# Rows of w_o loaded and split in a lane beside the gated unit, a tenth gate pair by seven products, and order and paces reset, in a hybrid S5 and mLSTM block

## The chip, the cores and the metric

The kernel runs on one core of a Trainium2 chip. The metric is the time of one execution on the device, in microseconds (us), taken as the median of several runs. Besides the runs there is one profiled execution, from which the page of the profile and all answers of the trace come. Engines are named as in the profile: PE (matmul), PEld (its weight loads), DVE (vector), ACT (scalar), POOL, SP (which issues most DMAs; SPq is its queue).

## The reference, cut to what matters

One decoder block on 1024 positions plus 16 learned meta positions, width 1024, all in float32:

```python
h = layer_norm(concat(meta, x))
p = h @ w_in + b_in        # u_s5 | q | k | v | o | i | f | g_s5 | g_m
y_s5 = GLU(gelu(S5(u_s5))) # z = gelu(y) @ s5_w_glu; z[:, :D] * sigmoid(z[:, D:])
y_m  = (sigmoid(o) * head_norm(mLSTM(q, k, v, i, f))) @ m_w_out
mix  = sigmoid(g_s5) * y_s5 + sigmoid(g_m) * y_m
h    = layer_norm(ALPHA * h + mix @ w_o)
h    = layer_norm(ALPHA * h + relu(h @ w_up + b_up)**2 @ w_down)
```

The output leaves out the meta positions.

## The kernel before, in words

Every product keeps float32 accuracy by splitting both operands into a high and a low part (type fp32r) and adding three matmuls: high by high (L274), low by high or high by low (L275, L276), in the helper `mm3`. A weight tile of 128x1024 (512 KB) is loaded by a DMA into `wraw`, copied on ACT to its high part (`whi`, rounded) and subtracted on DVE to its low part (`wlo`). All such tiles are slots of one pool, `big`, with 30 slots; a load can be issued only when the slot that it takes is free.

The program runs a list of jobs, one after the other on PE: first LN0 and the first jobs, in an order written out by hand; then those of the string `ORDER`. In it `q`, `v`, `u`, `o` are plain jobs of the first projection (`o0` to `o7` the output gate's tiles of 128 columns). The gates (o, g_s5, g_m) can also be taken in pairs of tiles by seven products in place of eight (Strassen's scheme in Winograd's form): pair p has a first part `a`p (`ga_job`, three products; ACT and DVE split the raw weights into `gmwh`/`gmwl`, DVE makes sums of weights, `wus`, at L1472 to L1475, of which one is split into `gmo`) and a second part `b`p (`gb_job`, four products). Between the two, weights' sums lie in DRAM (`gw_dr`) and partial results in `e_dr`, and are fetched again; only pairs that are among the last three `a` and the first three `b` stay in SBUF (`HELD`). Pairs 0 to 3 are the tiles of o, 4 to 7 those of g_s5, 8 to 11 those of g_m. `G_E` and `G_L` are lists of pairs whose split of the weights is written earlier, or whose third operand is written later.

After `ORDER` come `ym0` to `ym7` (the product with m_w_out) and `glu` to `glu7`, the gated unit, whose evacuation on ACT (`z2s`, L1087) and DVE (L1091 to L1093) ends in `mixr`. It reads two of the four batches of gelu(y) from rows 7 and 6 of the buffer `hT_hi`/`hT_lo` (`GROW`), which before held h transposed. Then comes the product with w_o: its eight rows of 128x1024 are loaded into `woraw` (L1606) and split into the eight rows of the same buffer (L1607 on ACT, L1608 on DVE); `mix` is split into `mxh` (L1620, ACT) and `mxl` (L1621, DVE), 64 pieces of 128x128 each; LN1 follows, then the feed-forward (up by seven products, down), and LN2.

Beside the jobs run lanes: generators for work that feeds other stages (mLSTM `ml`, S5 `s5`, `s5c`, `s5g`; the scaled residual `ah_scale`; the gate on the mLSTM's result `hm_gate`; the first up weights `up_early`, which writes split sums `wpre` and stores them in `wu_dr`). `LANE_AT` says at which job a lane begins, `PACE` how fast it goes against PE's clock, which `mm3` counts. In the S5 lane the 64 results `s5z` (64x130) go from PSUM to `s5Z` by ACT (L917) or DVE (L915); with `ZD = 1` every second one is on DVE. A scheduler then sets the final order of each engine from this program text.

Of the kernel before, what the change touches and what calls it, by code (L numbers as in the profile page):

```python
# [12 lines left out]
AF = mybir.ActivationFunctionType  # L13
OP = mybir.AluOpType
P = 128

D = 1024
KT = D // P
# [19 lines left out]
LN2_1 = 0.693359375  # L38
LN2_2 = math.log(2.0) - LN2_1
MAGIC = 1.5 * 2 ** 23  # L40
ORDER = 'q1 q0 v0 v1 q3 q2 o3 v2 a3 o0 u0 u1 v3 o2 o4 o5 u2 o1 a4 a6 a7 u3 a11 a8 a9 a5 a10 b9 b10 b5 b4 b3 b6 b8 b11 b7'
HS = 3
GH = 3
HOLD = 3
# [1 line left out]
TFA = 1  # L46
TLA = 1
T_UP = 100
REST = 11.83
G_E = [5, 10]  # L50
G_L = [5]
HGD = 1
UPD = 1
TPW = 5.29
S5_START = 'o3'
LANE_AT = {'t_prep': 'q0', 'hm_gate': 'a8', 'hmo': 'b7', 'ah_scale': 'ym5', 'up_early': 'glu3'}
PACE = {'ml': 0.56, 'cv': 0.104, 's5': 1.103, 's5c': 0.683, 's5g': 3.512, 'ah': 1.602, 'up': 1.036, 'hg': 1.92, 'hn': 1.0, 'hm': 0.66}
UP = {'ml': 10, 'cv': 0, 's5': 0, 's5c': 0, 's5g': 0, 'ah': 0, 'up': 0, 'hg': 0, 'hn': 0, 'hm': 0}
SPLIT_UP = 0
PRE = 3  # L60
UP_AT = (0, 1, 4, 6)
ZD = 1
ML = [1.912, 1.186, 1.815, 10.865]
NL = [0.584, 3.726, 10.192, 11.252]
B5 = [16, 0.1, 0.1, 50]
C5 = [0.84, 0.798, 1.345, 4.956]
K5 = [1.652, 1.0, 8.0, 0.475]
Z5 = [2.284, 1.264, 0.394, 0.269]
D5 = [3.696, 1.28, 1.716, 0.267]
W5 = [5.284, 0.829, 15.575, 0.848]  # L70
Y5 = [0.792, 1.657, 4.502, 6.57]
CV0 = 0
HRA = 1
A_AFT = 0
# [71 lines left out]
def decoder_block(  # L146
# [4 lines left out]
    nc = tc.nc  # L151
    v_, a_, g_, t_ = nc.vector, nc.scalar, nc.gpsimd, nc.tensor
# [9 lines left out]
    def slot(name, dt=F32):  # L162
        return big.tile([P, SLOT], dt, tag="s", name=name)
# [7 lines left out]
    def f32(ap):  # L171
        return ap.bitcast(F32)
# [3 lines left out]

    lanes = {n: Lane(p, tc, UP.get(n, 0)) for n, p in PACE.items()}
    clock = [0.0]
# [59 lines left out]
    def split_w(job, later=False):  # L238
        if later:
            return split_now(job, True)  # L240
        with tc.high_priority(offset=SPLIT_UP):
            split_now(job)
# [258 lines left out]
    def mlstm(h):  # L501
# [21 lines left out]
        def A(c):  # L523
            c0, n = chunk(c)
            if c < NCH - 1:
                ps = sdps("pk")
                t_.transpose(ps[:n, :DK], kT[:, c0:c0 + n], ident)
                kws[c] = mid.tile([P, DK], F32, tag="kw", bufs=2, name="kw")
                a_.activation(kws[c][:n], ps[:n, :DK], AF.Copy, scale=gB[:n, c0 + n - 1:c0 + n])
            if c > 0:  # L530
                ps = sdps("pS")
                t_.matmul(ps[:, :P], kT[:, c0:c0 + n], qT[:, c0:c0 + n], start=True, stop=True)
                sws[c] = mid.tile([P, P], F32, tag="sw", bufs=2, name="sw")
                v_.tensor_tensor(sws[c], ps[:, :P], gB[:, c0:c0 + n], op=OP.mult)
# [61 lines left out]
        for c in range(NCH):  # L596
            if c + 1 < NCH:
                A(c + 1)
            yield ML[h]
            B(c)  # L600
            yield ML[h]
            if c == 4:
# [190 lines left out]
    def s5_tables():  # L793
        E, bd = S5["E"], S5["bd"]
        for b in range(4):
            q0 = 4 * b
            yield B5[b]
            bt, wt = s5_in_load(b)
# [36 lines left out]
            nc.sync.dma_start(kt_dr[b], Kt)  # L835
            yield K5[b]
            Mi, tm = slot("s5Mi"), slot("s5tm")
# [56 lines left out]
    def s5_batch(b):  # L894
# [9 lines left out]
        for q in range(4):  # L904
# [5 lines left out]
            for g2 in range(2):  # L910
                for ri in range(2):
                    o = Z[64 * g2:64 * g2 + 64, ri * 520 + q * 130:ri * 520 + q * 130 + 130]
                    i = ps[64 * ri:64 * ri + 64, g2 * 130:g2 * 130 + 130]
                    if ri == ZD:
                        v_.tensor_copy(o, i)  # L915
                    else:
                        a_.activation(o, i, AF.Copy)  # L917
            yield Z5[b]
        c, s = T[:, 0:520], T[:, 520:1040]
# [3 lines left out]
        def ri(t, n):  # L923
            return t[:, 0:2 * n].rearrange("p (r c) -> p r c", r=2)
        for w, k in ((w1, c), (w2, s)):
            v_.tensor_tensor(ri(w, 520), ri(Z, 520), k[:, None, :].to_broadcast([P, 2, 520]), op=OP.mult)
        yield D5[b]
        v_.tensor_tensor(zr, w1[:, 0:520], w2[:, 520:1040], op=OP.add)
        v_.tensor_tensor(zi, w1[:, 520:1040], w2[:, 0:520], op=OP.subtract)
        for q in range(4):  # L930
            rq = S5["r8"][:, 4 * b + q:4 * b + q + 1].to_broadcast([P, NB])
            for z in range(2):
                o = z * 520 + q * NB
                v_.tensor_tensor_scan(w1[:, o:o + NB], rq, Z[:, o:o + NB], 0.0, op0=OP.mult, op1=OP.add)
        yield D5[b]

        x8 = w1[:, 0:1040].rearrange("p (r q c) -> p r q c", r=2, q=4)[:, :, :, 1:129]
        for o, k in ((Z, c), (w2, s)):
            v_.tensor_tensor(o[:, 0:1024].rearrange("p (r q c) -> p r q c", r=2, q=4), x8,
                             k.rearrange("p (q c) -> p q c", q=4)[:, None, :, 1:129].to_broadcast([P, 2, 4, P]),  # L940
                             op=OP.mult)
        yield D5[b]
        for i, op in enumerate((OP.subtract, OP.add)):
            for g2 in range(2):
                r = slice(64 * g2, 64 * g2 + 64)
                v_.tensor_tensor(w1[64 * i:64 * i + 64, 512 * g2:512 * g2 + 512], Z[r, 512 * i:512 * i + 512],
                                 w2[r, 512 - 512 * i:1024 - 512 * i], op=op)
        yield D5[b]
        if b + 1 < 4 and b + 1 in UD:
# [4 lines left out]
        for hf in range(2):  # L954
# [9 lines left out]
            a_.activation(Y[:, hf * 512:(hf + 1) * 512], ps, AF.Copy)  # L964
            yield Y5[b]
        nc.sync.dma_start(ys_dr[b].rearrange("p g c -> p (g c)"), Y[:, 0:1024])
        lanes["s5g"].add(s5_gelu(b))

    ROWS, GROW = set(), []
# [55 lines left out]
    def split_row(src, row):  # L1025
        hi, lo = hT_hi[:, row, 0:D], hT_lo[:, row, 0:D]
        a_.activation(hi, src[:, :D], AF.Copy)
        v_.tensor_tensor(lo, src[:, :D], f32(hi), op=OP.subtract)
        return hi, lo
# [71 lines left out]
    def t_prep():  # L1101
        for c in range(4):
            r = [slot("tpr"), slot("tpr")]
            for i in range(2):
                nc.sync.dma_start(r[i][:, :D], h_dr[c + 4 * i])
            yield TPW
            quarter_sums(r[0], r[1])
# [51 lines left out]
    def ga_prep(p):  # L1159
        def prep(raw):  # L1160
            r0, r1 = raw
            hi, lo = split_act(r0, "gmw") if p in G_E else (None, None)
            n1, n2 = wsums(r0[:, 0:512], r0[:, 512:1024], r1[:, 0:512], r1[:, 512:1024])
            if p in HELD:
                HELD[p] = [n1, r1]
            else:
                nc.sync.dma_start(gw_dr[p, 0], n1[:, :D])
                nc.sync.dma_start(gw_dr[p, 1], r1[:, :D])
            if p not in G_E:
                hi, lo = split_act(r0, "gmw")  # L1170

            def third():
# [4 lines left out]
            return {1: (hi[:, 0:512], lo[:, 0:512]), 2: (hi[:, 512:1024], lo[:, 512:1024]),  # L1177
                    3: third if p in G_L else third()}
        return prep
# [23 lines left out]
    def ga_job(p):  # L1203
        def run(job):
# [15 lines left out]
            elif p == TAIL[-1]:  # L1220
                lanes["s5"].at = max(lanes["s5"].at, clock[0] + REST)
                t_load(1)
# [224 lines left out]
    def ah_scale():  # L1447
# [4 lines left out]
        for t in range(9):  # L1452
# [12 lines left out]
                yield 1.5  # L1465
            nc.sync.dma_start(ah_dr[(t - 1) * P:t * P, :], r[:, :D])

    wu_dr = dram.tile([PRE, 7, P, 1024], F32, name="wu_dr")

    def wsums(a11, a12, a21, a22):  # L1470
# [34 lines left out]

    A_ALL = [int(w[1:]) for w in ORDER.split() if w[0] == "a"]
    TAIL = A_ALL[-3:]
    T_AT = A_ALL[-3 - TFA], A_ALL[-3 - TLA]
    HELD.update({p: None for p in [int(w[1:]) for w in ORDER.split() if w[0] == "b"][:HOLD] if p in TAIL})
    B_END = [int(w[1:]) for w in ORDER.split() if w[0] == "b"][-1]  # L1510

    for w in ORDER.split():
        n, i = w[0], int(w[1:])
# [26 lines left out]
    for w in LOAD0.split():  # L1540
        i = int(w[1])
# [24 lines left out]

    kinds = [w[0] for w in ORDER.split()]
    tail = max(i for i, w in enumerate(kinds) if w == "a") - 2
    assert all(w in "ab" for w in kinds[ORDER.split().index(f"a{TAIL[0]}"):])
    assert "b" not in kinds[:tail]  # L1570
    for i, j in enumerate(jobs):
        if j.raw is None and j.w is None:
            load_w(j)
        if j.w is None:
            split_w(j)
        if j.ran:
            next_split(jobs, i)
        for d in (1, 2):
            if i + d < len(jobs) and jobs[i + d].raw is None and jobs[i + d].w is None:
                load_w(jobs[i + d])  # L1580
        if j.tag == S5_START:
            lanes["s5c"].add(s5_pre())
            lanes["s5c"].add(s5_tables())
        for lane, name, gen in (("ah", "t_prep", t_prep), ("hg", "hm_gate", hm_gate), ("hm", "hmo", hmo_load),
                                ("ah", "ah_scale", ah_scale), ("up", "up_early", up_early)):
            if j.tag == LANE_AT[name]:
                lanes[lane].add(gen())
        if j.tag == "glu":
            for n in ("cv", "ml", "hn", "s5c", "s5", "s5g"):
                lanes[n].drain()  # L1590
            mid_ctx.close()
            ring_ctx = ExitStack()
            ring[0] = ring_ctx.enter_context(tc.tile_pool(name="ring", bufs=1, side="left"))
        j.run(j)
        j.w = j.plain = None
# [6 lines left out]
    ext = ext_ctx.enter_context(tc.tile_pool(name="ext", bufs=1, side="left"))  # L1602
    wo_hi, wo_lo = hT_hi, hT_lo
    for k in range(KT):
        r = slot("woraw")
        nc.sync.dma_start(r[:, :D], wo[k * P:(k + 1) * P, :])  # L1606
        a_.activation(wo_hi[:, k, :D], r[:, :D], AF.Copy)  # L1607
        v_.tensor_tensor(wo_lo[:, k, :D], r[:, :D], f32(wo_hi[:, k, :D]), op=OP.subtract)  # L1608

    MH, ACC, H1, RAW = {}, {}, {}, {}  # L1610
    res_dr = dram.tile([SEQ, D], F32, name="res_dr")
# [570 lines left out]
```

## Time and profile before

| what | value |
|---|---|
| runs | 1507.6, 1508.93, 1509.72 us; median 1508.93 |
| profiled execution | 1507.92 us, its span 1506.1 us |
| mean granted PE clock | 0.995 |
| busy share of the span | PE 99%, DVE 70%, ACT 43%, POOL 1% |
| DMA | 327.65 MB, mean 218 GB/s |

The profiled execution's time is its span and about 1.8 us around it. Busy shares are averages over all stages. In rows of the timeline the columns are the start in us from the beginning of the span, the busy us, the engine and line, the operation with the names of its output and inputs, and in brackets the idle time of that engine just before and what ended it. A name such as "mm L274 <- ACT hT_hi L1607" in the list of waits means that the matmul of line 274 waited for what ACT wrote to hT_hi in line 1607.

### The profile page before, as it was taken

Reading aid. Unit: us, or ns where it says so; the run is one execution under the profiler, and the core shown is the slowest. Engines: PE = TensorE matmul, PEld = TensorE weight load, DVE = VectorE, ACT = ScalarE, POOL = GpSimd, SP = SyncE. Lnnn points to the kernel's source line nnn. Section 1 sums busy time; section 2 is a strip of 40 time slices with the busy share of each in tenths; the row PEclk is TensorE's granted clock in tenths of the full one; section 3 lists DMA queues with packets and bytes.
Section 4 is the critical chain, followed back from the end, with each engine's and each line's share of the span. In section 5 each row is a group of like instructions: output and inputs, shape, how many; then the busy total and the mean of one; then the engine's idle time right before and its main releaser. Section 6 shows DMA issues by size and latency. Waiting matters only on the chain.

```text
span 1506.1 us, 20548 instructions
## 1 busy us (share of the span) xinstructions
PE 1484.5 (99%) x7522; PEld 1251.7 (83%) x7522; DVE 1061.1 (70%) x1914; ACT 644.9 (43%) x1022; POOL 22.1 (1%) x113
## 2 busy tenths in 40 slices
PE   9999999999999999999989999999999999999997
PEld 9999998988788888888868888888888888888886
DVE  8877778777677755445885676666666789767786
ACT  7523625443356466111462244444444624333340
POOL 0000000000000000000000011000000000000000
PEclk9999999999999999999989999999999999999999
DMA  8525236846968899776782267544443997767642
GB/s 331 204 95 186 71 112 215 239 148 216 307 232 315 291 372 368 270 258 247 282 307 84 70 182 243 178 152 154 144 145 125 328 395 244 239 224 236 212 178 102
DMA packets 131669, 327.65 MB, mean 218 GB/s; under 512 B 18464, under 2 KB 32864, under 8 KB 131568
## 3 DMA queue, kind: packets, MB, share of 16 engines
q1 hardware_dynamic: 128544, 315.32, 60.5%
q0 software_dynamic: 3024, 11.01, 2.4%
q8 instruction: 59, 0.97, 0.3%
q14 instruction: 42, 0.34, 0.1%
HBM read 214.90 MB, written 111.38 MB: 217 GB/s over the span
## 4 chain that ended last, share of the span: by engine, by line
PE 93%; DVE 3%; DMA 2%; ACT 2%; issue 1%; SPq 0%; DVEq 0%; ACTq 0%
PE mm L276 22%; PE mm L275 22%; PE mm L274 22%; PE sd L275 6%; PE sd L274 6%; PE sd L276 6%; PE mm L270 2%; PE mm L309 1%; PE pn L542 1%; PE pn L543 1%; PE pu L546 1%; DMA wu_dr<-wpre 1%; DMA wraw<-in_wf_dram 1%; PE ln L1663 0%; PE pt L586 0%
## 5 line engine op out<-in xcount | busy, mean ns | idle before, releaser
L274 PE MATMUL mm<-hT_hi,whi 128*128 128x512 f32 (+3 forms) x432 | 158.9, 369 | 0.0
L275 PE MATMUL mm<-hT_lo,whi 128*128 128x512 f32 (+3 forms) x432 | 158.3, 366 | 0.0
L276 PE MATMUL mm<-hT_hi,wlo 128*128 128x512 f32 (+3 forms) x432 | 158.1, 367 | 0.0
L275 PE MATMUL sd<-dwl,dah 128*128 128x512 f32 (+1 forms) x256 | 98.9, 386 | 0.0
L276 PE MATMUL sd<-dwh,dal 128*128 128x512 f32 (+1 forms) x256 | 98.6, 385 | 0.0
L274 PE MATMUL sd<-dwh,dah 128*128 128x512 f32 (+1 forms) x256 | 98.6, 386 | 0.0
L1872 ACT ACTIVATE dah<-da 128x1024 fp32r<-128x1024 f32 x56 | 58.6, 1052 | 84.8 <-PE sd L275 37.2
L1876 ACT ACTIVATE dwh<-wdr 128x1024 fp32r<-128x1024 f32 x56 | 58.9, 1053 | 82.6 <-DMA wdr<-in_wdn_dram 22.1
L274 PEld LDWEIGHTS mm<-hT_hi,whi 128*128 128x128 f32 x432 | 81.3, 188 | 11.0 <-issue 0.7
L275 PEld LDWEIGHTS mm<-hT_lo,whi 128*128 128x128 f32 x432 | 81.3, 188 | 10.9 <-issue 0.5
L276 PEld LDWEIGHTS mm<-hT_hi,wlo 128*128 128x128 f32 x432 | 81.2, 188 | 10.5
L274 PE MATMUL mm<-hT_hi,gmwh 128*128 128x512 f32 x216 | 86.8, 404 | 0.4 <-DVE gmx L1266 0.4
L275 PE MATMUL mm<-hT_lo,gmwh 128*128 128x512 f32 x216 | 85.1, 394 | 0.0
L276 PE MATMUL mm<-hT_hi,gmwl 128*128 128x512 f32 x216 | 84.9, 397 | 0.0
L1873 DVE TENSOR_TENSOR dal<-da,dah 128x1024 fp32r<-128x1024 f32 x56 | 68.1, 1219 | 19.5 <-ACT dah L1872 19.5
L274 PE MATMUL mm<-dwh,dah 128*128 128x512 f32 (+1 forms) x208 | 79.7, 384 | 0.0
L276 PE MATMUL mm<-dwh,dal 128*128 128x512 f32 (+1 forms) x208 | 79.6, 384 | 0.0
L275 PE MATMUL mm<-dwl,dah 128*128 128x512 f32 (+1 forms) x208 | 79.6, 384 | 0.0
L1877 DVE TENSOR_TENSOR dwl<-wdr,dwh 128x1024 fp32r<-128x1024 f32 x56 | 68.2, 1219 | 11.1 <-ACT dwh L1876 10.5
L276 PE MATMUL mm<-whi,hT_lo 128*128 128x256 f32 (+1 forms) x256 | 74.5, 291 | 0.0
L274 PE MATMUL mm<-whi,hT_hi 128*128 128x256 f32 (+1 forms) x256 | 73.3, 286 | 0.0
L275 PE MATMUL mm<-wlo,hT_hi 128*128 128x256 f32 (+1 forms) x256 | 72.8, 284 | 0.0
(472 smaller groups left out, 3773.5 us busy)
## 6 DMA issues: line engine op xcount, KB each, us to landing
da<-act_dr SPq DMA_DIRECT2D x56, 512.0 KB
wdr<-in_wdn_dram SPq DMA_DIRECT2D x56, 512.0 KB
wraw<-in_wf_dram SPq DMA_DIRECT2D x36, 512.0 KB
wur<-in_wup_dram SPq DMA_DIRECT2D x32, 512.0 KB
act_dr<-upy SPq DMA_DIRECT2D x64, 256.0 KB
wu_dr<-wpre SPq DMA_DIRECT2D x21, 512.0 KB
wpre<-wu_dr POOLq DMA_DIRECT2D x21, 512.0 KB, 5.5
act_dr<-upx SPq DMA_DIRECT2D x32, 256.0 KB
```

The costliest lines, as they stand in the source:

```text
L270: t_.matmul(ps, tm[i], tm[j], start=(w == 0 and k == 0), stop=(w == 2 and k == n - 1))
L274: t_.matmul(ps, ah, bh, start=(i == 0 and part[0]), stop=False, skip_group_check=skip)
L275: t_.matmul(ps, ah, bl, start=False, stop=False, skip_group_check=skip)
L276: t_.matmul(ps, al, bh, start=False, stop=(i == n - 1 and part[1]), skip_group_check=skip)
L309: t_.matmul(ps[:, :P], job.first[:, k * P:(k + 1) * P], HF[c0][:, k * P:(k + 1) * P], start=(k == 0), stop=(k == KT - 1))
L542: t_.matmul(pn[:, :258], qi[:, c0:c0 + n], Cs[c][:, :258], start=True, stop=False)
L543: t_.matmul(pn[:, :258], sws[c], vt[c][:, :258], start=False, stop=True)
L546: t_.matmul(pu[:, :258], kws[c][:n], vt[c][:n, :258], start=True, stop=True)
L1872: a_.activation(ah[:, :D], a[:, :D], AF.Copy)
L1873: v_.tensor_tensor(alo[:, :D], a[:, :D], f32(ah[:, :D]), op=OP.subtract)
L1876: a_.activation(wh, raw[i], AF.Copy)
L1877: v_.tensor_tensor(wl, raw[i], f32(wh), op=OP.subtract)
```

## The change

The change has three parts. First, a new lane, `wo`, begun at glu5, loads the rows of w_o that the gated unit does not read and splits them into the buffer; the loop after the gated unit does the rest. Second, `o4` and `o5` leave `ORDER` as plain jobs and become pair 2 by seven products (`a2`, `b2`), so that ten pairs are taken in this way in place of nine, and other pairs change places. Third, the numbers that set order and paces are other ones: `up_early` begins at glu1 in place of glu3, `ah_scale` at ym3 in place of ym5, `hm_gate` at u3 in place of a8, and all 64 copies to s5Z are on ACT (`ZD = 2`).

```diff
-ORDER = 'q1 q0 v0 v1 q3 q2 o3 v2 a3 o0 u0 u1 v3 o2 o4 o5 u2 o1 a4 a6 a7 u3 a11 a8 a9 a5 a10 b9 b10 b5 b4 b3 b6 b8 b11 b7'
+ORDER = 'q0 q1 v0 v1 q3 q2 o3 v2 a4 o0 u0 u1 v3 o2 u2 o1 a2 a3 a6 a7 u3 a11 a5 a8 a10 a9 b10 b9 b5 b2 b4 b6 b3 b8 b11 b7'
...
-G_E = [5, 10]
-G_L = [5]
+G_E = [9]
+G_L = [9]
...
-LANE_AT = {'t_prep': 'q0', 'hm_gate': 'a8', 'hmo': 'b7', 'ah_scale': 'ym5', 'up_early': 'glu3'}
+LANE_AT = {'t_prep': 'q0', 'hm_gate': 'u3', 'hmo': 'b7', 'ah_scale': 'ym3', 'up_early': 'glu1', 'wo': 'glu5'}
...
-ZD = 1
+ZD = 2
...
+    WO = set()
+
+    def wo_row_load(k):
+        r = slot("woraw")
+        nc.sync.dma_start(r[:, :D], wo[k * P:(k + 1) * P, :])
+        return r
+
+    def wo_row_split(k, r):
+        split_row(r, k)
+        WO.add(k)
+
+    def wo_early():
+        rs = {}
+        ks = [k for k in range(KT) if k not in GROW]
+        for i in range(len(ks) + 1):
+            if i < len(ks):
+                rs[i] = wo_row_load(ks[i])
+            if i > 0:
+                wo_row_split(ks[i - 1], rs.pop(i - 1))
+            yield 2.0
...
     for k in range(KT):
-        r = slot("woraw")
-        nc.sync.dma_start(r[:, :D], wo[k * P:(k + 1) * P, :])
-        a_.activation(wo_hi[:, k, :D], r[:, :D], AF.Copy)
-        v_.tensor_tensor(wo_lo[:, k, :D], r[:, :D], f32(wo_hi[:, k, :D]), op=OP.subtract)
+        if k not in WO:
+            wo_row_split(k, wo_row_load(k))
```

Besides these, `REST`, `TPW`, `PACE`, `UP` and one or two entries each of the lists `ML`, `B5`, `K5`, `Z5`, `D5`, `Y5` have new values.

What the scheduler makes of it stands in the order of the engines. On ACT, at the end of the gated unit, there stood before (z2s is the gated unit's sigmoid, wpre a copy for the up weights, hT_hi<-woraw the high part of a row of w_o):

```order
L1498 ACTIVATE wpre<-wur 128x512
L1087 ACTIVATE z2s<-mm 128x512 x2
L1620 ACTIVATE mxh<-mixr 128x128 x39
L1607 ACTIVATE hT_hi<-woraw 128x1024
L1620 ACTIVATE mxh<-mixr 128x128 x4
L1607 ACTIVATE hT_hi<-woraw 128x1024
L1620 ACTIVATE mxh<-mixr 128x128 x3
L1607 ACTIVATE hT_hi<-woraw 128x1024 x2
```

And on ACT at the same place of the changed program (L1027 is the split in `split_row`, L254 that of the gated unit's weights):

```order
L254 ACTIVATE whi<-wraw 128x1024
L1087 ACTIVATE z2s<-mm 128x512
L1027 ACTIVATE hT_hi<-woraw 128x1024 x3
L1087 ACTIVATE z2s<-mm 128x512
L1027 ACTIVATE hT_hi<-woraw 128x1024
L1640 ACTIVATE mxh<-mixr 128x128 x7
L1027 ACTIVATE hT_hi<-woraw 128x1024
L1640 ACTIVATE mxh<-mixr 128x128 x7
L1087 ACTIVATE z2s<-mm 128x512
L1027 ACTIVATE hT_hi<-woraw 128x1024
L1640 ACTIVATE mxh<-mixr 128x128 x26
L1027 ACTIVATE hT_hi<-woraw 128x1024
```

Six splits of rows of w_o moved ahead of or among the last sigmoids and the first mxh; the seventh row is behind 40 mxh, as the first one was.

On SP the loads of w_o stood behind all stores of the up weights and behind the gated unit's last loads:

```order
L1301 DMA mixr<-mix_dr 128x1024
L1302 DMA sgs<-sig_dr 128x1024
L1500 DMA wu_dr<-wpre 128x1024 x14
L1606 DMA woraw<-in_wo_dram 128x1024 x8
L1627 DMA acc<-ah_dr 128x1024 x3
```

Now the same queue reads:

```order
L1301 DMA mixr<-mix_dr 128x1024
L1521 DMA wu_dr<-wpre 128x1024 x2
L1302 DMA sgs<-sig_dr 128x1024
L1521 DMA wu_dr<-wpre 128x1024
L1472 DMA woraw<-in_wo_dram 128x1024
L1521 DMA wu_dr<-wpre 128x1024 x2
L1472 DMA woraw<-in_wo_dram 128x1024 x7
L1647 DMA acc<-ah_dr 128x1024 x3
```

The last stores moved in between the gated unit's last loads, and one load of w_o is ahead of two of them.

In the stretch of the gate pairs, DVE had the copies to s5Z among the sums of a pair's weights:

```order
L1472 TENSOR_TENSOR wus<-wraw 128x512
L915 COPY s5Z<-s5z 64x130 x3
L1473 TENSOR_TENSOR wus<-wus,wraw 128x512
L1474 TENSOR_TENSOR wraw<-wraw 128x512
L915 COPY s5Z<-s5z 64x130 x3
L1475 TENSOR_TENSOR wus<-wraw,wus 128x512
```

Now these copies are on ACT, which at that stage of the changed program has this order (gso and gme are evacuations of a gate pair, s5Y one of S5, kw one of the mLSTM):

```order
L564 ACTIVATE hraw<-pn,dd 128x256
L1192 ACTIVATE gso<-mm,bft 128x512
L964 ACTIVATE s5Y<-s5y 128x512
L529 ACTIVATE kw<-pk,gB 128x128
L964 ACTIVATE s5Y<-s5y 128x512
L1033 ACTIVATE gmwh<-wraw 128x1024
L1174 ACTIVATE gmo<-wus 128x512
L1186 ACTIVATE gme<-mm 128x512
L917 ACTIVATE s5Z<-s5z 64x130 x8
L1197 ACTIVATE gme<-mm 128x512
L917 ACTIVATE s5Z<-s5z 64x130 x4
```

The copies moved from DVE, where they came between the sums, to ACT, where they come in groups of four or eight between a pair's evacuations.

More of the change, by code (lines that the diff above doesn't have):

```diff
@@ L48 @@
 T_UP = 100
-REST = 11.83
-G_E = [5, 10]
-G_L = [5]
+REST = 11.24
+G_E = [9]
+G_L = [9]
 HGD = 1
 UPD = 1
-TPW = 5.29
+TPW = 3.48
 S5_START = 'o3'
-LANE_AT = {'t_prep': 'q0', 'hm_gate': 'a8', 'hmo': 'b7', 'ah_scale': 'ym5', 'up_early': 'glu3'}
-PACE = {'ml': 0.56, 'cv': 0.104, 's5': 1.103, 's5c': 0.683, 's5g': 3.512, 'ah': 1.602, 'up': 1.036, 'hg': 1.92, 'hn': 1.0, 'hm': 0.66}
-UP = {'ml': 10, 'cv': 0, 's5': 0, 's5c': 0, 's5g': 0, 'ah': 0, 'up': 0, 'hg': 0, 'hn': 0, 'hm': 0}
+LANE_AT = {'t_prep': 'q0', 'hm_gate': 'u3', 'hmo': 'b7', 'ah_scale': 'ym3', 'up_early': 'glu1', 'wo': 'glu5'}
+PACE = {'ml': 0.617, 'cv': 0.104, 's5': 1.103, 's5c': 0.683, 's5g': 3.753, 'ah': 2.202, 'up': 1.036, 'hg': 1.728, 'hn': 1.0, 'hm': 0.66, 'wo': 1.0}
+UP = {'ml': 10, 'cv': 0, 's5': 0, 's5c': 0, 's5g': -25, 'ah': 0, 'up': 0, 'hg': 0, 'hn': 0, 'hm': 0, 'wo': 0}
 SPLIT_UP = 0
@@ L61 @@
 UP_AT = (0, 1, 4, 6)
-ZD = 1
-ML = [1.912, 1.186, 1.815, 10.865]
+ZD = 2
+ML = [1.912, 1.186, 1.815, 7.605]
 NL = [0.584, 3.726, 10.192, 11.252]
-B5 = [16, 0.1, 0.1, 50]
+B5 = [16, 0.1, 0.1, 16]
 C5 = [0.84, 0.798, 1.345, 4.956]
-K5 = [1.652, 1.0, 8.0, 0.475]
-Z5 = [2.284, 1.264, 0.394, 0.269]
-D5 = [3.696, 1.28, 1.716, 0.267]
+K5 = [1.735, 1.0, 8.0, 0.665]
+Z5 = [1.941, 1.264, 0.749, 0.269]
+D5 = [3.696, 1.28, 2.025, 0.267]
 W5 = [5.284, 0.829, 15.575, 0.848]
-Y5 = [0.792, 1.657, 4.502, 6.57]
+Y5 = [0.792, 0.831, 4.502, 6.57]
 CV0 = 0
@@ L1584, in decoder_block @@
         for lane, name, gen in (("ah", "t_prep", t_prep), ("hg", "hm_gate", hm_gate), ("hm", "hmo", hmo_load),
-                                ("ah", "ah_scale", ah_scale), ("up", "up_early", up_early)):
+                                ("ah", "ah_scale", ah_scale), ("up", "up_early", up_early),
+                                ("wo", "wo", wo_early)):
             if j.tag == LANE_AT[name]:
```

## The prediction

> **What bounds the kernel now.** I read the profile's page first: busy time by engine and the chain that ended last.
>
> ```profile
> PE 1484.5 (99%) x7522; PEld 1251.7 (83%) x7522; DVE 1061.1 (70%) x1914; ACT 644.9 (43%) x1022; POOL 22.1 (1%) x113
> PE 93%; DVE 3%; DMA 2%; ACT 2%; issue 1%; SPq 0%; DVEq 0%; ACTq 0%
> ```
>
> TensorE (PE) is busy 99% of the span and holds 93% of the chain. So an edit pays only by taking matmuls away, or by closing one of the places where PE waits or runs below its rate. I looked for both: the rate in stretches of 40 us, the waits in PE's list of waits. The columns of a stretch are: its length, busy us (count) of PE, weight loads, DVE, ACT, POOL, then the granted PE clock, the DMA share, GB/s.
>
> ```profile
> 400.00:440.00 40.00, 37.65 (x194) 32.35 (x193) 32.01 (x65) 22.71 (x34) 0.00 (x0) 1.00 0.75 285
> 640.00:680.00 40.00, 40.00 (x174) 32.44 (x173) 17.57 (x18) 6.97 (x5) 0.00 (x0) 1.00 0.74 255
> 720.00:760.00 40.00, 40.00 (x175) 32.46 (x173) 37.24 (x59) 17.56 (x31) 2.30 (x4) 1.00 0.77 281
> 760.00:800.00 40.00, 34.21 (x131) 26.70 (x130) 28.75 (x83) 23.07 (x75) 0.00 (x0) 0.87 0.63 246
> ```
>
> From 640 to 680 all matmuls have 512 columns: 174 in 40 us, so 0.230 us each. From 760 to 800 there are 131 of the same width, 43 fewer, and 43 x 0.230 = 9.9 us are lost. That is the largest loss in the span, and it is the junction of the gated unit (glu0 to glu7) and the product with w_o. From 400 to 440, where the output gates' pairs lie beside the S5 convolution, PE stands 2.35 us. The list of PE's waits (total, times, longest) names what ended them:
>
> ```profile
> PE mm L274 <- ACT hT_hi L1607: 5.2, 1, 5.2
> PE mm L309 <- ACT hf L1396: 1.7, 2, 1.2
> PE s5z L907 <- DVE s5Z L915: 1.5, 1, 1.5
> ...
> PE pS L532 <- ACT hraw L564: 0.8, 1, 0.8
> PE mm L275 <- DVE hT_lo L1608: 0.6, 1, 0.6
> ```
>
> The 5.2 us are the first matmul of w_o, waiting for row 0 of w_o to be split. The timeline there (start, us, engine, instruction, wait before it):
>
> ```profile
> 765.02 6.47 SPq L1606 DMA_DIRECT2D woraw<-in_wo_dram  x5
> 767.36 6.51 ACT L1620 ACTIVATE mxh<-mixr 128x128 fp32r<-128x128 f32 x32 [1.23 <-DMA wu_dr<-wpre]
> 769.27 0.40 PE L276 MATMUL mm<-hT_hi,wlo 128*128 128x512 f32 x1
> 773.76 1.05 ACT L1607 ACTIVATE hT_hi<-woraw 128x1024 fp32r<-128x1024 f32 x1
> 774.87 2.50 PE L274 MATMUL mm<-hT_hi,mxh 128*128 128x512 f32 x5 [5.20 <-ACT hT_hi L1607]
> 776.68 1.22 DVE L1608 TENSOR_TENSOR hT_lo<-woraw,hT_hi 128x1024 fp32r<-128x1024 f32 x1
> ```
>
> PE ends the gated unit at 769.67. The split of row 0 stands on ACT behind the splits of the mix (mxh), and those had waited for slots that stores of the up weights (wu_dr) held. It runs at 773.76, PE starts at 774.87, and the low half on DVE comes at 776.68 and makes a second wait of 0.6. The rest of the 9.9 us is the clock:
>
> ```profile
> 770.00:772.00 2.00, 0.00 (x0) 0.00 (x0) 2.00 (x8) 2.00 (x12) 0.00 (x0) 1.00 1.03 416
> 772.00:774.00 2.00, 0.00 (x0) 0.00 (x0) 2.00 (x10) 2.00 (x11) 0.00 (x0) 0.89 1.02 410
> 774.00:776.00 2.00, 1.14 (x3) 0.95 (x4) 2.00 (x9) 1.83 (x6) 0.00 (x0) 0.50 1.02 416
> 780.00:782.00 2.00, 2.00 (x7) 1.52 (x6) 2.00 (x7) 2.00 (x8) 0.00 (x0) 0.50 1.03 408
> 782.00:784.00 2.00, 2.00 (x7) 1.56 (x6) 2.00 (x6) 2.00 (x7) 0.00 (x0) 0.55 0.31 125
> 784.00:786.00 2.00, 2.00 (x10) 1.65 (x9) 2.00 (x8) 2.00 (x7) 0.00 (x0) 1.00 0.00 0
> ```
>
> The granted clock falls to 0.50 shortly before 774, about 4 us into the idle time, and is back only near 784: some 10 us at half rate. So 9.9 = 5.2 + 0.6 of waits + 4.1 of slow matmuls.
>
> **The change, part by part, against the profiled execution's 1507.92 us** (span 1506.1; the median of the runs is 1508.93, 1.0 above it).
>
> *The lane for w_o.* In the new order rows 0 to 5 of w_o are loaded while glu5 to glu7 run on PE, and their splits stand on ACT partly ahead of the last sigmoids (z2s), partly among the first 14 mxh, where before 39 mxh stood ahead of row 0; rows 6 and 7, which the gated unit reads to its end, come after it. The up weights' copies (wpre), begun at glu1 in place of glu3, all stand ahead of glu5's sigmoids, so their stores, the releaser of the 1.23 us above, end sooner too. The splits cost ACT 6 x 1.05 and DVE 6 x 1.22 us, the same work as before, only earlier. On SP the eight loads (512 KB, 1.3 us each at the 410 GB/s above) pass only the last two stores; the gated unit's loads stay ahead, those of LN1's residual (acc) behind, as before. A load that waits for a slot holds up acc alone, which is first asked for when a block of the result is done. DVE is the tight one: 37.24 of 40 us from 720 to 760. But the up weights' part of that moves two glu blocks, some 22 us, ahead into
>
> ```profile
> 680.00:720.00 40.00, 40.00 (x175) 32.48 (x174) 24.41 (x31) 8.15 (x12) 0.00 (x0) 1.00 0.70 249
> ```
>
> where DVE has 15.6 us free. What is late next is the low half of row 6. Ahead of it on DVE stand operations of these two rows (the second counts 15 of them, 10.3 us in all, 688 ns each):
>
> ```profile
> 767.80 1.10 DVE L1621 TENSOR_TENSOR mxl<-mixr,mxh 128x128 fp32r<-128x128 f32 x5 [0.19 <-ACT mxh L1620]
> L1091 DVE TENSOR_TENSOR z2s<-mm,z2s 128x512 f32<-128x512 f32 x15 | 10.3, 688 | 11.8 <-ACT z2s L1087 8.2 <-PE mm L276 3.6
> ```
>
> In the new order DVE has, between the end of the gated unit and that half, 26 mxl x 0.22, four operations of 0.69 for the mix and two splits x 1.22: 10.9 us. PE asks for it after 63 matmuls of w_o, 63 x 0.230 = 14.5 us. So I take the waits and the half clock as gone, -9.9. At worst 3 us of them stay; more than 9.9 can't go, since PE is then at its rate.
>
> [...]
>
> *Pair 2 of the output gates by seven products* (o4 and o5 become a2 and b2). 96 matmuls of 512 columns become 84: -12 x 0.230 = -2.8 us, all on PE, and certain as far as no wait takes it back. It adds on DVE four sums of 512 columns (0.69 each) and a few in the second part, and 12 transfers of 512 KB (8 for weights' sums, 4 for partial results, since eight pairs instead of six are stored and fetched again), 6.3 MB. At the 410 GB/s seen above this is 15.3 us of all DMA engines. The room for it:
>
> ```profile
> 400.00:560.00 160.00, 157.27 (x757) 130.79 (x756) 116.44 (x193) 92.51 (x131) 0.96 (x1) 1.00 0.86 307
> 560.00:600.00 40.00, 40.00 (x173) 32.35 (x172) 21.22 (x23) 23.11 (x27) 0.00 (x0) 1.00 1.00 371
> ```
>
> 160 us at a share of 0.86 leave 22 us, and at a share of 1.00 from 560 to 600 PE loses nothing. Cost between 0 (spread over the room) and 15.3 (all of it where the share is full); I take 0, since PE stood well even at the full share.
>
> *S5 copies and the reset order.* ZD = 2 puts all 64 s5Z copies on ACT, of which DVE had 32 (0.71 for three below, so some 8 us off DVE and 8 onto ACT). They were in the 1.5 us wait (the first row is for the size of ACT's 512-column work):
>
> ```profile
> 395.52 0.60 ACT L1197 ACTIVATE gme<-mm 128x512 f32<-128x512 f32 x1
> 401.99 0.69 DVE L1472 TENSOR_TENSOR wus<-wraw 128x512 f32<-128x512 f32 x1 [5.51 <-DMA wraw<-in_wf_dram]
> 402.72 0.71 DVE L915 COPY s5Z<-s5z 64x130 f32<-64x130 f32 x3
> 405.11 0.69 PE L907 MATMUL s5z<-s5U,s5Mi 128*128 128x130 f32 x4 [1.50 <-DVE s5Z L915]
> ```
>
> DVE stood 5.51 us behind a late weight (it is a queue in order), the copies behind it, and PE behind the copies. Copies on ACT don't stand behind that sum any more, so this wait goes. What is late next is ACT: in the new order a2, a3, a6, a7 come in a row there, and the split of a pair's weights (gmwh, 1.05 like the other splits of 1024 columns) stands there behind hraw, gso, kw and two s5Y copies of some 0.6 each. By these sizes I estimate waits of 0.4 and 1.2 to 2.5 us in that part of the program, against the 1.5, the 0.8 and smaller ones of the old one. Between -3 (all waits of the middle gone) and +6 (four pairs in a row with one wait of 1.5 each); I take 0, nearest to the one wait that the rows show.
>
> *Paces* (ah_scale at ym3, hm_gate at u3, others) move DVE and ACT work inside stretches where PE loses nothing (640 to 760 above): 0, between -1 and +2. The exchange of q0 and q1 at the start: 0.
>
> Sum: 1507.92 - 9.9 - 2.8 + 0 + 0 = 1495.2, so **1495**. The likeliest case runs from 1491.5 to 1498.5.
>
> **Rivals.**
> *A, the middle gives some back.* Four gate pairs in a row keep DVE (four sums each) and ACT as dense as the one at 400 us. For it: PE's 2.35 us there with one pair. Against: the copies leave DVE. Four waits of 1.5 us: 1495 + 6 = 1501.
> *B, the junction only changes its wait.* DVE, full to 37.24 of 40 before the junction, gets the lane's splits too; row 0's low half or the mix's splits are then late, and PE stands again. Under 4 us the clock holds and the case ends near 1498; over 4 us the half clock comes back as well, 1503 to 1506. For it: DVE is at 2.00 of 2.00 from 770 to 786. Against: the order, in which the sums of the up weights are off DVE sooner.
> *C, slower.* The loads of the gate pairs fall behind: the 5.51 us wait of DVE for wraw, once the 6.3 MB are added in a stretch that is already at 0.86, grows into one long wait on PE. Place: a2 to a7. Price: up to the 15.3 us of the added transfers, and 4 to 5 us for the half clock, which a wait over 4 us brings. That is 1495 + 15.3 + 5 = 1515. It decides from a delay of some 12 us on, since 1495 + 12 + 5 = 1512 is 3 past the median. Against: 22 us of room, and loads that are issued pairs ahead.
> *D, no effect*: the lane's loads start too late, as w_o's slots come free only with the last glu rows, and the middle takes back the 2.8: 1506 to 1509. The order speaks against it, since the loads stand before the last up stores.
> *E, better*: no wait in the middle either: 1495 - 3 - 1 = 1491, or a little under.
>
> **How the numbers follow.** Forecast 0.62 (1495); A 0.13 (1501); B 0.10 (1498 to 1506); C 0.05 (1515); D 0.05 (1507); E 0.05 (1491). The range 1491 to 1502 leaves out C, D, the worse half of B and a little at each end, about 0.2. What a measurement of this kernel can tell from no change is 0.2%, 3 us. Faster than 1505.9: the forecast, A, E, nearly all of B and a little of D, 0.89; within 0.2%: most of D, and a little of B and C, 0.06; slower: C, 0.05.
>
> **What would show it.** The wait for hT_hi at w_o's first matmul is gone from PE's list or under 1 us; the granted clock is 1.00 throughout the junction, and the 40 us around it hold 172 or more matmuls of 512 columns. No wait for DVE's s5Z is left; in its place stand waits of PE for gmwh or hraw of 3 us or less in all. The number of PE instructions falls by about 12. The forecast is wrong if the junction shows a wait over 3 us, or the stretch of a2 to a7 loses over 5 us of PE's time, with wraw or gmwh as releaser.

## The result, and the profile after

The changed kernel takes 1492.14 us (median of 5 runs, 1491.74 to 1493.64) against 1508.93 (5 runs, 1506.98 to 1509.72); the ratio is 0.9894 with an interval of 0.988 to 0.9908. That is inside the forecast range, 2.9 us under the forecast of 1495. Its profiled execution is its slowest run, 1493.64 us with a span of 1491.9, so the traces differ by 14.2 us in span where the medians differ by 16.8.

The page of the changed kernel, busy time and the chain that ended last:

```profile
PE 1479.2 (99%) x7510; PEld 1248.5 (84%) x7510; DVE 1056.3 (71%) x1892; ACT 657.4 (44%) x1059; POOL 22.3 (1%) x113
PE 98%; DVE 1%; ACT 1%; DMA 0%; issue 0%; SPq 0%; DVEq 0%
```

PE has 12 instructions fewer, and the chain is PE to 98%, in place of 93%. The whole list of PE's waits is now:

```profile
PE mm L309 <- ACT hf L1396: 1.7, 2, 1.2
PE warm L1415 <- DVE ident L188: 1.4, 1, 1.4
PE mm L270 <- ACT hT_hi L1404: 0.9, 1, 0.9
PE pS L532 <- ACT kw L529: 0.5, 1, 0.5
```

All four were there before. The junction's waits are gone, and so is every wait of the gate pairs' stretch. The stretches of 40 us show the same (PE is the first pair of numbers after the length):

```profile
400.00:440.00 40.00, 40.00 (x209) 35.08 (x209) 36.30 (x72) 22.37 (x37) 0.00 (x0) 1.00 1.00 379
740.00:780.00 40.00, 40.00 (x174) 32.38 (x173) 34.48 (x88) 25.02 (x78) 2.29 (x4) 1.00 0.59 225
```

From 740 to 780, with the junction in the middle, PE runs 174 matmuls at a clock of 1.00. From 400 to 440 it stands no more, at a DMA share of 1.00. The junction in the timeline of the changed kernel:

```profile
737.78 8.19 SPq L1472 DMA_DIRECT2D woraw<-in_wo_dram  x7
748.99 2.94 ACT L1027 ACTIVATE hT_hi<-woraw 128x1024 fp32r<-128x1024 f32 x3
764.80 0.40 PE L276 MATMUL mm<-hT_hi,wlo 128*128 128x512 f32 x1
765.04 0.39 PE L274 MATMUL mm<-hT_hi,mxh 128*128 128x512 f32 x1
772.75 1.21 DVE L1028 TENSOR_TENSOR hT_lo<-woraw,hT_hi 128x1024 fp32r<-128x1024 f32 x1
```

Rows 0 to 2 are split 13 us ahead of their use; the first matmul of w_o follows the last one of the gated unit with no gap. The low half of row 6 is ready at 773.96, 8.9 us after w_o's first matmul, where PE asks for it after 14.5.

To see where each kernel spends its time, I cut the traces at four marks that the timeline of PE shows: the first matmul mm<-hT_hi,whi (start), the first one that reads gelh (the gated unit begins), the first mm<-hT_hi,mxh (w_o begins), and the first one that reads h1h (the feed-forward begins). All in us:

| kernel | start | jobs and y_m | gated unit, with the wait at its end | w_o and LN1 | rest of the span | median time |
|---|---|---|---|---|---|---|
| before | 28.4 | 652.3 | 94.2 | 99.9 | 631.3 | 1508.93 |
| changed | 29.4 | 646.7 | 88.9 | 95.3 | 631.5 | 1492.14 |
| e1 changed, no lane | 27.8 | 646.3 | 88.8 | 95.2 | 630.3 | 1490.35 |
| e2 before, lane | 29.8 | 653.0 | 88.9 | 95.2 | 631.6 | 1498.31 |
| e3 before, up_early at glu1 | 31.7 | 652.7 | 88.6 | 95.5 | 632.4 | 1499.42 |
| e10 changed, neither of the two | 28.1 | 646.2 | 94.4 | 98.6 | 630.7 | 1499.99 |
| e7 changed, row 0 late | 26.9 | 646.2 | 91.7 | 100.0 | 632.0 | 1500.39 |
| e9 changed, ZD = 1 | 27.5 | 658.3 | 89.1 | 95.3 | 632.0 | 1503.43 (e4) |
| e5 changed, pair 2 plain | 27.8 | 665.3 | 89.0 | 95.3 | 631.2 | 1509.9 |
| e6 before, pair 2 by seven | 27.1 | 671.0 | 94.8 | 98.9 | 632.7 | 1528.82 |
| e8 changed, pair 1 by seven too | 28.2 | 674.4 | 89.0 | 95.3 | 630.3 | 1519.0 |
| e11 changed, paces of before | 29.6 | 662.8 | 89.0 | 95.3 | 630.5 | 1508.97 |
| e12 before, new paces and copies | 27.4 | 663.0 | 97.0 | 97.9 | 631.9 | 1518.47 |

Between before and changed, the start gives +1.0 (it differs from one execution to the next by up to 5 us), the jobs -5.6, the gated unit with its wait -5.2, w_o with its half clock -4.6, the rest +0.2. The junction is worth 9.8 us, the jobs 5.6. Two of e4's eight runs were slow (2090.46 and 2979.03 us), and its ratio leaves them out.

### The profile page after: what moved, and what is told of

Its sections match the earlier page's. It is cut to its first block, busy times and chain, and to the rows that moved or that the text cites. A ratio compares the mean times of both kernels' runs of the same rounds, so it can differ in the third digit from the quotient of the medians.

```text
span 1491.9 us, 20548 instructions
## 1 busy us (share of the span) xinstructions
PE 1479.2 (99%) x7510; PEld 1248.5 (84%) x7510; DVE 1056.3 (71%) x1892; ACT 657.4 (44%) x1059; POOL 22.3 (1%) x113
## 2 busy tenths in 40 slices
DMA packets 133686, 333.94 MB, mean 224 GB/s; under 512 B 18689, under 2 KB 33089, under 8 KB 133585
## 4 chain that ended last, share of the span: by engine, by line
PE 98%; DVE 1%; ACT 1%; DMA 0%; issue 0%; SPq 0%; DVEq 0%
PE mm L274 24%; PE mm L276 24%; PE mm L275 23%; PE sd L276 6%; PE sd L275 6%; PE sd L274 6%; PE mm L270 2%; PE mm L309 1%; PE pn L542 1%; PE pn L543 1%; PE pu L546 1%; PE s5z L907 0%; PE s5y L961 0%; PE s5y L960 0%; PE ln L1683 0%; PE pS L532 0%
## 5 line engine op out<-in xcount | busy, mean ns | idle before, releaser
L274 PE MATMUL mm<-hT_hi,whi 128*128 128x512 f32 (+3 forms) x400 | 145.6, 365 | 0.0
L276 PE MATMUL mm<-hT_hi,wlo 128*128 128x512 f32 (+3 forms) x400 | 145.6, 365 | 0.0
L275 PE MATMUL mm<-hT_lo,whi 128*128 128x512 f32 (+3 forms) x400 | 145.5, 364 | 0.0
L275 PE MATMUL sd<-dwl,dah 128*128 128x512 f32 (+1 forms) x256 | 98.9, 386 | 0.0
L274 PE MATMUL mm<-hT_hi,gmwh 128*128 128x512 f32 x240 | 96.0, 403 | 0.0
L275 PE MATMUL mm<-hT_lo,gmwh 128*128 128x512 f32 x240 | 95.2, 397 | 0.0
L276 PE MATMUL mm<-hT_hi,gmwl 128*128 128x512 f32 x240 | 94.8, 398 | 0.0
L274 PEld LDWEIGHTS mm<-hT_hi,whi 128*128 128x128 f32 x400 | 75.2, 188 | 10.3 <-issue 1.2
L275 PEld LDWEIGHTS mm<-hT_lo,whi 128*128 128x128 f32 x400 | 75.3, 188 | 9.5 <-issue 0.4
L276 PEld LDWEIGHTS mm<-hT_hi,wlo 128*128 128x128 f32 x400 | 75.2, 188 | 9.4
L1897 DVE TENSOR_TENSOR dwl<-wdr,dwh 128x1024 fp32r<-128x1024 f32 x56 | 68.1, 1218 | 17.7 <-ACT dwh L1896 17.1
L1893 DVE TENSOR_TENSOR dal<-da,dah 128x1024 fp32r<-128x1024 f32 x56 | 68.1, 1218 | 16.8 <-ACT dah L1892 16.8
```

The source lines that it names most:

```text
L274: t_.matmul(ps, ah, bh, start=(i == 0 and part[0]), stop=False, skip_group_check=skip)
L275: t_.matmul(ps, ah, bl, start=False, stop=False, skip_group_check=skip)
L276: t_.matmul(ps, al, bh, start=False, stop=(i == n - 1 and part[1]), skip_group_check=skip)
L1893: v_.tensor_tensor(alo[:, :D], a[:, :D], f32(ah[:, :D]), op=OP.subtract)
L1897: v_.tensor_tensor(wl, raw[i], f32(wh), op=OP.subtract)
```

## The experiments

The kernel before was run again beside each group of experiments: its median was 1508.1 us beside e1, e2, e3 and e7, 1508.0 beside e4, e5, e6 and e8, and 1507.0 beside e9 to e12. The ratios are against these.

**e1, e2, e3, e10: what closes the junction?** Two parts of the change act there: the lane, and up_early at glu1.

e1, the changed kernel without the lane:

```diff
-..., 'up_early': 'glu1', 'wo': 'glu5'}
+..., 'up_early': 'glu1', 'wo': 'none'}
```

> The changed kernel without the lane for w_o: all eight rows are loaded and split by the loop after the gated unit; up_early stays at glu1. Theory 1 (the lane itself closes the junction): the wait and the half clock come back, 1492 + 9.9 = 1502 us, with a wait for hT_hi of 4 us or more. Theory 2 (the up weights' copies, which end before glu5 now, had been what held row 0 back; the lane adds little): the loop finds ACT and the queue free and the time is 1492 to 1495, with a wait under 3 us and the clock at 1.00.

Measured: 1490.35 us (ratio 0.9887, 0.9874 to 0.99); the interval overlaps the changed kernel's, so the lane's own worth is not told from zero. Theory 1 fell. The junction has neither wait nor half clock:

```profile
740.00:780.00 40.00, 40.00 (x174) 32.47 (x173) 29.73 (x71) 25.14 (x78) 2.29 (x4) 1.00 0.55 204
734.87 9.20 SPq L1472 DMA_DIRECT2D woraw<-in_wo_dram  x8
755.23 1.05 ACT L1027 ACTIVATE hT_hi<-woraw 128x1024 fp32r<-128x1024 f32 x1
762.89 0.63 PE L274 MATMUL mm<-hT_hi,mxh 128*128 128x512 f32 x2
```

(The first row is the stretch, the others the timeline of e1.) The scheduler itself puts the loop's loads 28 us ahead of PE's need, as soon as the stores of the up weights are out of SP's queue, and row 0's split ends 6.6 us ahead.

e3, the kernel before with `'up_early': 'glu1'` alone:

> The kernel before with up_early at glu1 in place of glu3 and nothing else. Theory 1: row 0 still stands behind 14 mxh on ACT and its load is still late, so most of the wait stays: 1503 to 1507 us. Theory 2: 25 mxh fewer ahead of row 0, 25 x 0.2 = 5 us, take the wait to under 1 us, the clock stays at 1.00, and the time is 1508.5 - 9 = 1499 to 1500.

Measured: 1499.42 us (0.9946, 0.9932 to 0.9959), as theory 2 has it. e2, the kernel before with the lane alone (up_early at glu3):

> The kernel before with the lane for w_o at glu5 and nothing else; up_early stays at glu3. Theory 1: the junction closes, 1508.5 - 9.9 = 1498.6 us. Theory 2: the lane's splits share ACT and DVE with the up weights' copies, so that the mix's splits or rows come late; PE still waits 2 to 5 us and the time is 1502 to 1508.

Measured: 1498.31 us (0.994, 0.9928 to 0.9953), as theory 1 has it. So either one closes the junction by itself. The loads of w_o on SP, and w_o's first matmul, in the kernel before, in e2 and in e3:

```profile
737.79 20.48 SPq L1500 DMA_DIRECT2D wu_dr<-wpre  x14
758.36 13.13 SPq L1606 DMA_DIRECT2D woraw<-in_wo_dram  x8
```

```profile
738.51 0.33 SPq L1472 DMA_DIRECT2D woraw<-in_wo_dram  x1
771.70 0.40 PE L274 MATMUL mm<-hT_hi,mxh 128*128 128x512 f32 x1
```

```profile
748.98 6.39 SPq L1606 DMA_DIRECT2D woraw<-in_wo_dram  x8
768.17 2.90 ACT L1620 ACTIVATE mxh<-mixr 128x128 fp32r<-128x128 f32 x14
770.98 1.05 ACT L1607 ACTIVATE hT_hi<-woraw 128x1024 fp32r<-128x1024 f32 x1
773.03 1.08 PE L274 MATMUL mm<-hT_hi,mxh 128*128 128x512 f32 x4
```

Before, SP issued 14 stores of up weights over 20 us, with the loads behind them in its queue. The lane puts loads between the stores; the earlier start has the stores done sooner. On ACT, which came last before, row 0's split stands behind 14 mxh in e3 in place of 39, as theory 2 counted, and ends 1.0 us ahead of PE's matmul. That matmul carries no wait in e2 and e3. e10 takes both away from the changed kernel (`'up_early': 'glu3', 'wo': 'none'`):

> The changed kernel without the lane for w_o and with up_early at glu3 as before; order, pairs, copies and paces as changed. If either the lane or the earlier start closes the junction and nothing else does, both gone bring the wait of 5 us and the half clock back: 1491 + 9.9 = 1501 us. If the junction had been closed by the other parts: 1492.

Measured: 1499.99 us (0.9956, 0.9944 to 0.9968). The wait and the half clock are back, 7.9 us over the changed kernel:

```profile
PE mm L274 <- ACT hT_hi L1027: 5.4, 1, 5.4
740.00:780.00 40.00, 34.21 (x136) 26.87 (x135) 35.06 (x90) 27.14 (x84) 2.29 (x4) 0.91 0.83 312
```

In e10 the stretch loses 174 - 136 = 38 matmuls, 8.7 us. So no other part of the change closes the junction, and one of the two was enough.

**e7: does a shorter wait bring the half clock?** The lane leaves out row 0:

```diff
-        ks = [k for k in range(KT) if k not in GROW]
+        ks = [k for k in range(1, KT) if k not in GROW]
```

> The changed kernel with row 0 of w_o left to the loop after the gated unit; the other five rows stay in the lane. PE needs row 0 first, and on ACT its split now stands behind 35 mxh, so PE waits about 3 us (35 x 0.2 us of mxh against the 5.5 us of the last half of the gated unit, then 1.05 for the split and the low half on DVE). If the clock falls only in an idle time of about 4 us or more: 1492 + 3 to 4 = 1495 to 1496 us with the clock at 1.00. If a shorter wait brings the half clock too: 1499 or more.

Measured: 1500.39 us (0.9949, 0.9937 to 0.9961). The second answer is right: a shorter wait, 2.64 us, brings the half clock too. PE in the timeline, and stretches of 2 us:

```profile
764.87 1.80 PE L274 MATMUL mm<-hT_hi,mxh 128*128 128x512 f32 x5 [2.64 <-ACT hT_hi L1027]
769.10 0.79 PE L275 MATMUL mm<-hT_lo,mxh 128*128 128x512 f32 x1 [2.43 <-DVE hT_lo L1028]
```

```profile
762.00:764.00 2.00, 0.22 (x1) 0.00 (x0) 2.00 (x8) 2.00 (x11) 0.00 (x0) 1.00 0.00 0
764.00:766.00 2.00, 1.13 (x4) 0.95 (x5) 2.00 (x10) 2.00 (x8) 0.00 (x0) 0.93 0.00 0
766.00:768.00 2.00, 0.67 (x2) 0.00 (x0) 2.00 (x7) 2.00 (x8) 0.00 (x0) 0.50 0.02 4
772.00:774.00 2.00, 2.00 (x9) 1.61 (x8) 2.00 (x6) 0.95 (x5) 0.00 (x0) 0.87 0.01 2
```

The half clock runs from about 765.7 (0.93 from 764 to 766) to 772.5. PE's first wait, 2.64 us, had ended at 764.87, and its second, 2.43 us, began at 766.67, five matmuls later. So the first wait by itself brought the clock down, and the second fell into the half clock.

**e4 and e9: the copies.** The changed kernel with `ZD = 1`:

> The changed kernel with ZD = 1: every second copy to s5Z on DVE again, all else as changed. Theory 1 (the copies on DVE had made the waits of the gate pairs' stretch): a wait for DVE's s5Z of 1 to 2 us is back, 1492 + 1.5 to 3 = 1493.5 to 1495 us. Theory 2 (the new order of the pairs took the waits away): no such wait, 1492 within 1 us.

Measured: 1503.43 us (0.9971, 0.996 to 0.9982), 11 us more than the changed kernel: nearly four times what theory 1 gave at most. e9 is the same kernel once more, for its profile.

> The changed kernel with ZD = 1 once more, for its profile: its time was 1503.4 us, 11 us over the changed kernel's. If the 32 copies on DVE alone cost that, PE waits for DVE's s5Z, 11 us in all, in the stretch of the gate pairs. If the copies shift the order of all later work there (the scheduler's), the waits stand on other names too (gmwh, gmo, gme, s5w, C), and their sum is about 11 us.

Measured: 1503.97 us in one run, 11.6 more in the jobs than in the changed kernel. Its waits, a stretch of 2 us, and DVE, ACT, PE in the timeline:

```profile
PE mm L274 <- ACT gmo L1174: 2.8, 2, 2.0
PE s5y L961 <- DVE s5w L946: 2.0, 1, 2.0
```

```profile
378.00:380.00 2.00, 2.00 (x5) 1.61 (x6) 2.00 (x5) 0.78 (x2) 0.95 (x1) 0.50 0.93 274
```

```profile
373.86 2.65 DVE L934 TENSOR_TENSOR_SCAN s5w<-s_r,s5Z 128x130 f32<-128x130 f32 x8
376.43 0.67 DVE L1496 TENSOR_TENSOR wus<-wraw,wus 128x512 f32<-128x512 f32 x1
377.18 0.63 ACT L1174 ACTIVATE gmo<-wus 128x512 fp32r<-128x512 f32 x1 [2.63 <-DVE wus L1496]
377.86 0.73 PE L274 MATMUL mm<-hT_hi,gmo 128*128 128x512 f32 x1 [2.04 <-ACT gmo L1174]
```

No wait for s5Z is in the list. The last sum of a pair's weights stands on DVE behind S5's scan; ACT's gmo waits 2.63 us for it, and PE 2.04 for gmo. It is the second answer: with the copies back on DVE, the rest of S5's work falls elsewhere among the pairs' work. The waits that the changed kernel does not have come to 7.2 us. The half clock adds to them: it stands twice for 3.4 us in e9's jobs, each time after one wait of 2.0 us. At a granted clock of 0.50 the matmuls of 512 columns come 0.43 us apart (e7, 770.12 to 772.25), at 1.00 0.23, a rate of 0.54; by that I estimate that PE loses 3.1 of these 6.8 us, which with the 7.2 makes 10.3 of the 11.6.

**e5, e6, e8: a pair more or less.** e5, the changed kernel with o4 and o5 plain:

```diff
-... u2 o1 a2 a3 a6 a7 ... b5 b2 b4 ...
+... u2 o1 o4 o5 a3 a6 a7 ... b5 b4 ...
```

> The changed kernel with o4 and o5 as plain jobs again at the place of a2, and without b2: nine pairs. Theory 1: 12 matmuls of 0.230 us come back, 1492 + 2.8 = 1494.8 us. Theory 2 (sums and transfers of the tenth pair cost PE some of what it saves): less, 1492 to 1493.5.

Measured: 1509.9 us (1.0015, 1.0007 to 1.0024), 17.8 us more, of which 2.8 are matmuls. e6, the kernel before with `o4 o5` out and `a2`, `b2` in:

> The kernel before with pair 2 by seven products and nothing else: a2 in the place of o4 and o5 (after u2 and o1), b2 after b5. Theory 1: 12 matmuls fewer, 1508.1 - 2.8 = 1505.3 us, with the waits of the middle as they were. Theory 2: with before's paces and copies the added sums and transfers make new waits of PE, 1507 us or more.

Measured: 1528.82 us (1.0147, 1.0131 to 1.0164), 20.8 us slower than before. e8, an eleventh pair in the changed kernel (o2, o3 become a1, b1):

> The changed kernel with an eleventh pair by seven products: o2 and o3 become a1 (before a2) and b1 (before b2); the S5 lane begins at v2 in place of o3. If DVE, ACT and the transfers have room for one more pair: 12 matmuls fewer, 1492 - 2.8 = 1489 us. If the stretch of the pairs is full (DMA share 0.89 to 1.00 from 360 to 560 us, 6.3 MB more): waits for wraw or gmwh take it back, 1492 or more.

Measured: 1519.0 us (1.0071, 1.0059 to 1.0083). Neither theory had the size of any of the three. The longest waits of e5, of e6 and of e8:

```profile
PE s5z L907 <- DMA s5Mi<-mi_dr: 3.2, 1, 3.2
PE mm L274 <- DVE gme L1259: 2.8, 2, 1.5
PE mm L274 <- ACT gmwh L1033: 2.2, 1, 2.2
```

```profile
PE s5y L961 <- DVE s5w L946: 6.5, 1, 6.5
...
PE mm L276 <- DVE gmwl L1034: 3.7, 1, 3.7
```

```profile
PE mm L274 <- ACT gmwh L1033: 4.6, 2, 4.2
PE mm L274 <- ACT gmo L1174: 3.4, 2, 2.0
```

By these names it is the meeting of S5 or the mLSTM with the pairs' preparation again, at other places, whether a pair is added or taken away; no run takes these waits away one by one. The clock falls with them: the granted clock is 0.50 for 10.2 us in e5's jobs, 13.7 in e6's and 17.1 in e8's, and never in those of before and of the changed kernel. In e5 the new waits (10.6 us), 4.7 of the 10.2 us (an estimate by the same rate of 0.54) and the 2.8 of matmuls make 18.1 of the 18.6 us that the jobs take longer.

**e11, e12: the paces.** e11, the changed kernel with before's REST, TPW, PACE, UP, ML, B5, K5, Z5, D5, Y5:

> The changed kernel with REST, TPW, PACE, UP and the lists ML, B5, K5, Z5, D5, Y5 as before; order of jobs, pairs, copies, lanes' places as changed. If the paces only move work inside stretches that have room (the prediction's zero): 1492 within 2 us. If the paces and the order of the jobs belong together: waits of PE on gmwh, gmo, gme or S5's names from 360 to 560 us, 1500 us or more.

Measured: 1508.97 us (1.0008, 0.9999 to 1.0017): the paces alone are worth 16.8 us in the new order. Its longest waits:

```profile
PE pn L542 <- DVE sw L534: 4.3, 1, 4.3
PE mm L274 <- ACT gmo L1174: 2.8, 1, 2.8
```

e12, the kernel before with the new values of these and ZD = 2:

> The reverse: the kernel before with the new REST, TPW, PACE, UP, lists and ZD = 2, its order of jobs, pairs and the junction as before. If paces and copies alone take the waits of the middle away: 1508.1 - 3.5 = 1504.6 us. If they belong to the new order of jobs: new waits, 1510 us or more.

Measured: 1518.47 us (1.0075, 1.0063 to 1.0087), 11.5 us slower than before; 10.7 of it lies in the jobs, and the wait at the junction grew to 8.0. So the old paces are bad for the new order, and the new paces, together with all copies on ACT, are bad for the old one; which of these two costs the most there was not tried.

## Why the prediction was right, and where its steps were not

*The sum.* Forecast 1507.92 - 9.9 - 2.8 + 0 = 1495.2; the profiled execution gave 1493.64, the median 1492.14. The likeliest case's junction came true to 0.1 us (9.8 by the table). The matmuls: 12 fewer on the page of the profile, 2.8 us. What was off is the middle: it was put at 0 and is worth another -2.8 (the jobs' -5.6 less the 2.8). The waits that stood there before, 1.5 us for s5Z, 0.8 for hraw and 0.4 for gmx, make 2.7 of it. No wait is left there now, which is the condition of rival E, put at 0.05, while the rest came as forecast.

*The middle's step that failed* is the estimate of waits of 0.4 and 1.2 to 2.5 us for gmwh. It counted what stands ahead of gmwh on ACT and not what stands ahead of its user on PE. The changed kernel's timeline there:

```profile
389.30 1.79 PE L907 MATMUL s5z<-s5U,s5Mi 128*128 128x130 f32 x12
389.77 1.05 ACT L1033 ACTIVATE gmwh<-wraw 128x1024 fp32r<-128x1024 f32 x1
390.88 0.50 PE L274 MATMUL mm<-hT_hi,gmwh 128*128 128x512 f32 x1
```

The split ends at 390.82, and PE, busy with S5's twelve s5z until then, takes it at 390.88. At this pair S5's matmuls cover the pair's preparation, to within 0.1 us.

*The lane.* The size was right, the credit was not. The step named both the lane and the earlier up weights and gave the lane the 9.9; e1, e2, e3 and e10 show that each alone is enough. Of rival D's two conditions neither came: the loads went out 27 us ahead.

*The paces* were costed at 0, between -1 and +2, "inside stretches where PE loses nothing". As a term of its own that was wrong by far (e11: 16.8 us; the new places of ah_scale and hm_gate, which that term names too, were not undone by themselves). They move the work of S5 and of the mLSTM among the gate pairs, not only between 640 and 760. The terms of the middle don't add up one by one: copies, pair and paces singly undone cost 11, 18 and 17 us, while all together gain 5.6. The sum came near because order and paces came together. That these fit each other was read from no row, so it is luck that the middle came near 0. The junction and the matmuls were not luck.

*Rivals.* A, B and C did not come; the changed kernel moves 333.94 MB in place of 327.65, 6.3 more, and PE loses nothing even at a DMA share of 1.00 from 400 to 440. The 4 us at which B and C let the clock fall were my estimate, from the one fall in the trace of before, about 4 us into its wait of 5.2; they are too many: the clock fell after one wait of 2.64 us (e7) and after one of 2.04 (e9). In e7 the clock was back 3.4 us after PE's second wait ended (769.10 to 772.5), where before it took 5.8 us from the end of PE's last wait (777.95 to 783.8).

## What to carry to other kernels

Where a stall at a stage's beginning has two remedies, try each by itself: here an earlier start of the queue's other customers did what the new lane does, in one number. In a kernel whose lanes are paced against an order of jobs, an edit to the order is not to be priced by its own instructions alone: the changed kernel was 17 us slower with the old paces, 11 with half of the copies back on DVE, and 18 without its tenth pair. And for a wait, look at what stands ahead of the user on its own engine, not only at the queue of the one it waits for. A wait of 2 us can cost more than 2 us, since the clock may fall behind it (e9: after 2.04 us of waiting, 3.41 us at 0.50); so look at the granted clock beside each wait.

## What the runs showed of the hardware that was not expected

One idle time of PE of 2.64 us set the clock to 0.50 about 3.5 us after it began, and the clock stayed there for 6.8 us, over a second idle time of 2.43 (e7). By the table, waits and clock together cost 7.5 us (91.7 + 100.0 against 88.9 + 95.3) for 5.1 us of waiting; the one wait of 5.2 us before, with a second of 0.6, cost 9.8.

The length of a wait does not settle by itself whether the clock falls. Within e5, PE's wait of 2.16 us leaves it at 1.00, and after a shorter one of 1.94 us it stands at 0.50 (for "issue" the profile names no releaser):

```profile
466.93 0.50 PE L274 MATMUL mm<-hT_hi,gmwh 128*128 128x512 f32 x1 [2.16 <-ACT gmwh L1033]
468.00:470.00 2.00, 2.00 (x10) 1.63 (x9) 1.97 (x5) 0.31 (x1) 0.00 (x0) 1.00 1.02 355
515.65 0.46 PE L960 MATMUL s5y<-s5U,s5Mx 128*128 128x128 f32 x2 [1.94 <-issue]
518.00:520.00 2.00, 2.00 (x6) 1.56 (x5) 2.00 (x4) 0.08 (x1) 0.00 (x0) 0.50 1.04 410
```

From 480 to 520 PE is idle for 6.6 us in e5, at a mean clock of 0.87, so these rows alone do not tell which wait brought the 0.50. e9 has a shorter wait by itself, 2.04 us up to 377.86: the clock is 1.00 from 374 to 376, 0.99 from 376 to 378 and 0.50 from 378 to 380.

By the clock in the traces, between their start and their end, the half clock lasted 3.41 us twice in e9, 6.83 in e7, e10 and e11, and 10.24 before: one, two and three times 3.41. What sets these lengths no run here shows.
